# State space parameters in seventeen small steps, and the state space inputs in sixteen transfers

## Chip, core and metric

The kernel runs on one core of a Trainium2 chip. The metric is the device time of one execution in microseconds (us). Before the change the median of three runs is 3636.02 us (3635.19 to 3643.21).

The engines are named as the profile names them: PE is TensorE (matmuls and transposes), PEld its weight loads, DVE is VectorE, ACT is ScalarE, POOL is GpSimd, SP is SyncE, which in this kernel issues every DMA.

## The reference

512 tokens of width 2048 pass through two layers of a first block and one layer of a second block. The change touches only the first block. Each of its layers computes, from x and a condition vector c:

```python
mod = c_act @ w_ada[l] + b_ada[l]                     # shift, scale, gate
h = rms_norm(x, norm_g[l]) * (1 + scale) + shift
u, z_s, q, k, v, z_a = split(h @ w_in[l])             # six parts of width 1024
y_s = s5_mixer(u, ...) * silu(z_s)                    # state space part
y_a = diff_attention(rope(q), rope(k), v) * silu(z_a)
x = x + gate * (concat(y_s, y_a) @ w_out[l])
```

The state space part is a linear recurrence with 64 groups of 16 channels and 64 complex states each:

```python
step = exp(log_step); a_bar = exp(lam * step)
b_bar = ((a_bar - 1) / lam)[..., None] * b_mat
states = scan(a_bar, einsum('gnp,bsgp->bsgn', b_bar, u))
y = einsum('gpn,bsgn->bsgp', c_mat, states).real + d_skip * u
```

followed by a gelu and a gated linear unit. What depends on parameters alone (powers of `a_bar`, their products with B and C) is computed on the chip in each layer, and that computation is what the change moves.

## The kernel before

**Weights.** All large products are fp32 done as three matmuls of a high and a low part. `piece` (L261) loads 512 KB of weights into one of five `raw` buffers, ACT rounds it to `hi` (L266), DVE makes `lo = raw - hi` (L269), and `mm3` or `group_tok` issues 24 matmuls of 512 columns for it: 8 of `hi` with the high activations, 8 of `hi` with the low ones, 8 of `lo`. `piece` also calls, at a set rate, a filler that loads a piece of `w_ada` into `raw` and reduces it on DVE (L515, the "dots").

**Order.** The program is written in the order of priority. A planner then simulates the engines and gives each engine, and the queue of SP, a fixed order of instructions: at each point the instruction of highest priority that is ready by its estimates. On the chip every engine works through its list in order, so one that is late there holds up all behind it, transfers in SP's queue too.

**Layer 0.** `start` computes `u` of layer 0 (pieces of `wuA0`, then, after the loop over `before`, four pieces of `wuB0`) and writes it to DRAM as `u_d`. Then eight pieces of `za` (gate of the attention), eight pieces of `wv` (values, `group_tok`), and eight heads: a block for q (two pieces), one for k, the attention. State space steps are put beside the heads. Layer 1 has the same parts, with `za` in eight blocks of two pieces.

**Parameters** (`ssm_params`). A scalar part (about a hundred DVE instructions on 32 columns) is followed by four quarters `qd`. Each quarter loads its B and C from DRAM (`ssb`, L653) into the one buffer `g[:, 1536:2048]`, and then
- DVE makes `E`, powers times B, in 24 instructions (`powmul`, L664 to L666), into one of two halves of `G[:, 0:8]`;
- POOL negates a part of C (L673), clears `Cb` and copies C into it (L676, L679);
- PE multiplies `Cb` with `E` (L685, 32 small matmuls) into a bank `kp` with tag `tr`; ACT copies it (L688), PE transposes it back into `kp` (L690), DVE copies and completes it (L693 to L699) and eight DMAs store it (`K_d`, L702);
- PE transposes `E` (L708, 16 of them, into the two banks of tag `tr`), ACT copies, four DMAs store (`FT_d`);
- POOL makes `CA`, powers times C, in 24 instructions (again L664 to L666), and four DMAs store it (`CA_d`).

The next quarter's load overwrites the buffer that `CA` reads, and in program order each quarter's POOL work stands behind the one before. `Cb`, `ks`, `k2` and the copies of the transposes share four buffers of tag `p`. In layer 0 the scalar part is called after `start`, and one quarter after each second piece of `za` (`beside`). The parameters of layer 1 are all called at once in layer 0 (`mid`), between the gated linear unit (`glu`) and the output product (eight pieces of `woA`, ten blocks of `wo`, then half blocks).

**Inputs** (`ssm_steps`). Eight DMAs read `u_d` in rows of 64 numbers (256 bytes) into `up = G[:, 0:8]` (L762), all at the first step, which is called after `za` and before `wv`. `E` uses the same part of `G`. Then come eight state steps, which load `FT_d` (L769) into two alternating halves and run 16 matmuls each (L776), the recurrence on POOL (L788 to L791), and eight output steps.

Of the kernel before, what the change touches and what calls it, by code (L numbers as in the profile page):

```python
# [20 lines left out]
KT = 16  # L21
# [146 lines left out]
class Kern:  # L168
# [150 lines left out]

    def group(self, srcs, ns, acts, evac, extra=(), rate=None, halves=0):  # L320


        nk = len(acts)
        pss = [self.bank() for _ in range(4)] + [self.sbank(t, b) for t, b in extra]
        for c, k0 in [(c, k0) for c in HALVES for k0 in range(0, halves, 2)] + [(slice(0, S), k0) for k0 in range(halves, nk, 2)]:
            if k0 == max(halves, 4) and rate is not None:
                self.rate = rate
            base = 0
            for src, n in zip(srcs, ns):
                w = n * 128  # L330
                hi, lo = self.piece(src[:, k0 * w:(k0 + 2) * w], 2 * w)
                self.mm3([(pss[base + m][:, c], slice(k * w + m * 128, k * w + (m + 1) * 128), [a[:, c] for a in acts[k0 + k]],
                           k0 + k == 0 and c.start == 0, k0 + k == nk - 1) for k in range(2) for m in range(n)], hi, lo)
                base += n
        for m in range(base):
            evac(m, pss[m])

    def group_tok(self, src, acts, n, evac, halves=0):

        nk = len(acts)  # L340
        pss = [self.bank() for _ in range(4)]
        per = 1024 // n // 2 * 2
        for tt, k0 in [(tt, k0) for tt in ((0, 1), (2, 3)) for k0 in range(0, halves, per)] + [(range(4), k0) for k0 in range(halves, nk, per)]:
            hi, lo = self.piece(src[:, k0 * n:(k0 + per) * n], per * n)
            for k in range(per):
                mh, ml = acts[k0 + k]
                sl = slice(k * n, (k + 1) * n)
                for t in tt:
                    ts = slice(t * 128, (t + 1) * 128)
                    first, last = k0 + k == 0, k0 + k == nk - 1  # L350
# [3 lines left out]
                    mm(pss[t][:, :n], ml[:, ts], hi[:, sl], start=False, stop=last)  # L354
        for t in range(4):
            evac(t, pss[t])
# [215 lines left out]
    def ssm_params(self, l):  # L572

        nc, I = self.nc, self.I
        g = self.G[:, 8:16, :].rearrange("p a b -> p (a b)")
# [53 lines left out]
        for i in range(4):  # L629
            t = pw[i]  # L630
# [16 lines left out]
        nc.vector.tensor_copy(cf[:, 96:128], ci)  # L647
        T = nc.gpsimd.tensor_tensor
        yield
        for qd in range(4):  # L650
            pa = slice(qd * 8, qd * 8 + 8)
            sbq = g[:, 1536:2048].rearrange("p (k r a c) -> p k r a c", k=2, r=2, a=8)
            nc.sync.dma_start(sbq.rearrange("p k r a c -> p (k r) (a c)"),  # L653
                              I[f"ssb{l}"].rearrange("p (k q c) -> p k q c", k=4, q=4)[:, :, qd])
            sc = self.t2("wt", 1, shape=(128, 1280))
            tm = sc[:, 0:512], sc[:, 512:1024]
            tv = self.t2("n", 4), self.t2("n", 4)

            def powmul(T, tm, out, f, src, n, op=ADD):

                fv = f.rearrange("p (k r a) -> p k r a", k=2, r=2)[:, :, :, pa]
                for r in range(2):
                    t = tm[r][:, :8 * n].rearrange("p (a c) -> p a c", a=8)
                    T(t, fv[:, 1, r].unsqueeze(2).to_broadcast([128, 8, n]), src[:, 1 - r], MUL)  # L664
                    T(out[:, r], fv[:, 0, r].unsqueeze(2).to_broadcast([128, 8, n]), src[:, r], MUL)
                    T(out[:, r], out[:, r], t, op)  # L666
            V = nc.vector.tensor_tensor
            E = self.G[:, 4 * (qd % 2):4 * (qd % 2) + 4, :].rearrange("p a b -> p (a b)").rearrange("p (r a dc) -> p r a dc", r=2, a=8)
            powmul(V, tv, E[:, :, :, 0:16], cf, sbq[:, 0], 16)
            for i, n in enumerate((16, 32, 64)):  # L670
                powmul(V, tv, E[:, :, :, n:2 * n], pw[i], E[:, :, :, 0:n], n)

# [7 lines left out]
            kp = self.sbank("tr", 2)  # L680
# [6 lines left out]
            ks, k2 = self.t2("p", 4), self.t2("p", 4)  # L687
            nc.scalar.copy(k2[:, :256], kp[:, :256])  # L688
            for x in range(2):
                nc.tensor.transpose(kp[:, 256 + 128 * x:384 + 128 * x], k2[:, 128 * x:128 * x + 128], self.ident)  # L690
# [12 lines left out]

            for r in range(2):
                for a0 in range(0, 8, 4):
# [5 lines left out]
                    nc.sync.dma_start(self.FT_d[l][qd * 2 + a0 // 4, r], ft)  # L711

            CA = g[:, 2048:4096].rearrange("p (r a ic) -> p r a ic", r=2, a=8)
            powmul(T, tm, CA[:, :, :, 0:16], pw[0], sbq[:, 1], 16, SUB)
            for i, n in enumerate((16, 32, 64)):
                powmul(T, tm, CA[:, :, :, n:2 * n], pw[i], CA[:, :, :, 0:n], n, SUB)
            for r in range(2):
                for h in range(2):
                    nc.sync.dma_start(self.CA_d[l][qd][64 * r:64 * r + 64, h], CA[64 * h:64 * h + 64, r])
            yield  # L720

    def ssm_param_storage(self):
# [8 lines left out]
        self.K_d = [self.dp.tile([16, 64, 15, 16], F32, name=f"K_d{l}") for l in range(2)]  # L731
        self.u_d = self.dp.tile([1024, 512], F32, name="u_d")

    def ssm_pad(self):
# [19 lines left out]
    def ssm_steps(self, l):  # L754
# [8 lines left out]
        yield  # L763

# [159 lines left out]

    def start(self, hacts, before):

# [28 lines left out]
        for m in range(4):  # L955
            self.ssm_put(m, pa[m], A[:, m, :])
        pb = [self.bank() for _ in range(4)]
        for k0 in (8, 10, 12, 14):
# [4 lines left out]

    def layer(self, l, xsrc, on_x, nxt, after_u=lambda: None, mid=lambda: None, beside=lambda: None):
        nc, I, A, G = self.nc, self.I, self.A, self.G
# [7 lines left out]
        def ev_za(j, ps):  # L973
            self.act(A[:, 8 + j, :], ps, AF.Silu)
        if l:
            self.blocks([wi[24 + j] for j in range(8)], hacts, ev_za)
        else:
            for j in range(8):
# [8 lines left out]
        ssm = self.ssm_steps(l)  # L987
        next(ssm)
        va = A[:, 0:4, :]
        self.group_tok(I[f"wv{l}"][0], hacts, 512, lambda t, ps: nc.scalar.copy(va[:, t, :], ps))  # L990

# [32 lines left out]
        self.rate = (1, 1)[l]  # L1024
        mid()
        yacts = [(self.HH[:, k, :].bitcast(F32R), self.HL[:, k, :].bitcast(F32R)) for k in range(16)]

        def ev_o(m, ps):
            nc.sync.dma_start(A[:, m, :], xsrc[m])
            self.stt(A[:, m, :], ps, self.mod[l][:, 32 + m:33 + m], A[:, m, :], MUL, ADD)  # L1030
            on_x(m)

        def ev_half(m, ps, c):
# [3 lines left out]
            on_x(m, c)  # L1037
        self.group([I[f"woA{l}"]], [4], yacts, ev_o)
        self.blocks([I[f"wo{l}"][j] for j in range(10)], yacts, lambda j, ps: ev_o(4 + j, ps))
        self.rate = 0  # L1040
# [497 lines left out]
def build(ctx, tc, I, O):  # L1538
# [22 lines left out]
    K.start(K.acts(), before)  # L1561
    next(par)
    K.ssm_pad()
    K.rope_tables()
    K.lambdas()
    K.gain_root()
    xs = K.dp.tile([2, KT, 128, 512], F32, name="xs")
# [63 lines left out]

    def mid():
        for _ in K.ssm_params(1):
            pass
    K.layer(0, [I["xT"][m] for m in range(KT)], on_x(0), nxt(0), after_u, mid, lambda: next(par, None))
    K.layer(1, [xs[0, m] for m in range(KT)], on_x(1), nxt(1))
# [18 lines left out]
```

## Time and profile before

| | before |
|---|---|
| median of three runs | 3636.02 us |
| the profiled execution | 3646.28 us |
| its span, first to last instruction | 3644.5 us |
| mean granted TensorE clock, of full speed | 0.969 |
| PE busy | 3442.2 us (94%) |
| DVE busy | 2118.7 us (58%) |
| ACT busy | 1187.5 us (33%) |
| POOL busy | 645.0 us (18%) |

Busy times of the engines overlap. The profiled execution lies 0.3% above the median of the runs, and 1.8 us of it lie outside the span. PE is nearly always busy, so time is gained where PE waits, and where its clock is granted at less than full speed.

### The profile page before, as it was taken

The page shows a single profiled execution, that of the slowest core. Times are in us where ns is not written, and L with a number is a line of the kernel's source. Part 1 is how long each engine was busy: PE and PEld are TensorE (multiplying, and loading weights), DVE is VectorE, ACT ScalarE, POOL GpSimd, SP SyncE. Part 2 cuts the span into 40 slices and gives each one's busy share as a digit, 9 for nine tenths or more (in the row PEclk, how much of TensorE's full clock was granted, in tenths as well). Part 3 has the DMA queues.
Part 4 walks back from the last instruction along what each step waited for, and adds up shares of the span by engine and source line. Part 5 has one row for each costly group of instructions (what it writes and reads, how often), then busy time and mean ns, then how long its engine had stood idle before and what let it go on. Part 6 is the DMA issues. An engine that isn't in the chain of part 4 may idle for free.

```text
span 3644.5 us, 45627 instructions
## 1 busy us (share of the span) xinstructions
PE 3442.2 (94%) x16673; PEld 2740.3 (75%) x16673; DVE 2118.7 (58%) x4157; ACT 1187.5 (33%) x2052; POOL 645.0 (18%) x885
## 2 busy tenths in 40 slices
PE   7987899999779998899999999999999999999999
PEld 4866667778569876677788887887888777788887
DVE  7983555667857334646575589823893246434432
ACT  3422232353124222323433344321532134433311
POOL 0064293001750003920002202000210000000000
PEclk8998999999889999999999999999999999999999
DMA  9856636656566855356577636332333232224442
GB/s 329 286 161 166 187 107 172 193 179 218 176 201 220 220 176 164 112 161 190 172 221 229 196 118 130 113 96 75 101 99 113 72 95 79 70 93 136 145 138 93
DMA packets 264862, 565.04 MB, mean 155 GB/s; under 512 B 76476, under 2 KB 113597, under 8 KB 264637
## 3 DMA queue, kind: packets, MB, share of 16 engines
q1 hardware_dynamic: 264638, 562.14, 50.6%
q8 instruction: 131, 2.15, 0.2%
q14 instruction: 93, 0.76, 0.1%
HBM read 497.89 MB, written 50.50 MB: 150 GB/s over the span
## 4 chain that ended last, share of the span: by engine, by line
PE 58%; DVE 9%; DMA 8%; POOL 4%; issue 3%; SPq 1%; ACT 0%; DVEq 0%; POOLq 0%; ACTq 0%
PE pp L281 16%; PE pp L282 16%; PE pp L284 16%; DMA raw<-in_wada 6%; DVE lo L269 2%; DVE G L249 1%; PE sc L888 1%; DVE raw L515 1%; DVE G L1232 1%; POOL G L791 1%; PE sc L1363 1%; POOL misc L789 1%; PE tr L1290 1%; POOL G L666 1%; SPq L804 1%
## 5 line engine op out<-in xcount | busy, mean ns | idle before, releaser
L281 PE MATMUL pp<-HH,hi 128*128 128x512 f32 (+1 forms) x3568 | 1401.5, 396 | 27.1 <-ACT HH L565 20.9
L282 PE MATMUL pp<-HL,hi 128*128 128x512 f32 (+1 forms) x3440 | 1345.5, 394 | 0.2 <-DVE HL L252 0.2
L266 ACT CAST hi<-raw 128x1024 fp32r<-128x1024 f32 (+1 forms) x538 | 560.5, 1043 | 1196.1 <-PE pp L282 973.8
L284 PE MATMUL pp<-HH,lo 128*128 128x512 f32 (+1 forms) x3568 | 910.9, 393 | 4.9 <-DVE lo L269 4.9
L269 DVE TENSOR_TENSOR lo<-raw,hi 128x1024 fp32r<-128x1024 f32 (+1 forms) x506 | 625.7, 1239 | 355.7 <-PE pp L284 174.7
L281 PEld LDWEIGHTS pp<-HH,hi 128*128 128x128 f32 x3568 | 682.5, 192 | 186.2 <-issue 28.6
L284 PEld LDWEIGHTS pp<-HH,lo 128*128 128x128 f32 x3568 | 663.1, 190 | 157.3 <-issue 18.6
L282 PEld LDWEIGHTS pp<-HL,hi 128*128 128x128 f32 x3440 | 658.0, 191 | 150.5 <-issue 20.2
L515 DVE CUSTOM_DVE_ANT_0 raw<-raw,cs,vec 128x1024 f32<-128x1024 f32 x112 | 155.3, 1388 | 265.1 <-DMA raw<-in_wada 252.7
L515 DVE CUSTOM_DVE_ANT_0 raw<-raw,cs,mod 128x1024 f32<-128x1024 f32 x112 | 146.5, 1308 | 246.9 <-DMA raw<-in_wada 228.4
L217 ACT ACTIVATE p<-p,st 128x128 f32<-128x128 f32 (+2 forms) x192 | 101.9, 531 | 232.0 <-DVE st L244 231.5
L1606 POOL TENSOR_TENSOR rp<-rp,n 128x512 f32<-128x512 f32 (+1 forms) x43 | 65.0, 1526 | 418.2 <-ACT n L1605 418.1
L353 PE MATMUL pp<-lo,HH 128*128 128x512 f32 (+1 forms) x320 | 123.2, 390 | 4.1 <-DVE lo L269 4.1
L352 PE MATMUL pp<-hi,HH 128*128 128x512 f32 (+1 forms) x320 | 122.3, 388 | 3.9 <-ACT HH L565 3.1
L269 POOL TENSOR_TENSOR lo<-raw,hi 128x1024 fp32r<-128x1024 f32 x32 | 77.9, 2434 | 255.5 <-PE pp L284 133.7
L354 PE MATMUL pp<-hi,HL 128*128 128x512 f32 (+1 forms) x320 | 117.3, 388 | 0.9 <-DVE HL L252 0.9
L788 POOL TENSOR_TENSOR misc<-misc,G 128x64 f32<-128x64 f32 x124 | 53.8, 434 | 330.4 <-ACT G L778 321.2
L888 PE MATMUL sc<-rp,rp 64*128 64x512 f32 (+3 forms) x256 | 89.9, 500 | 15.3 <-DVE st L890 15.3
L282 PE MATMUL pp<-A,hi 128*128 128x512 f32 x256 | 100.7, 393 | 0.0
L664 POOL TENSOR_TENSOR wt<-G 128x128 f32<-128x128 f32 (+2 forms) x64 | 65.4, 1041 | 174.9 <-DVE G L631 149.4
L890 DVE CUSTOM_DVE_ANT_0 p<-sc,cst 128x128 f32<-128x128 f32 (+3 forms) x128 | 60.8, 483 | 29.3 <-PE sc L888 29.2
L353 PEld LDWEIGHTS pp<-lo,HH 128*128 128x128 f32 x320 | 63.0, 197 | 18.4 <-DVE lo L269 4.7
(319 smaller groups left out, 3959.8 us busy)
## 6 DMA issues: line engine op xcount, KB each, us to landing
raw<-in_wada SPq DMA_DIRECT2D x224, 512.0 KB, 4.2
raw<-in_w SPq DMA_DIRECT2D x164, 512.0 KB, 3.8
raw<-in_win SPq DMA_DIRECT2D x128, 512.0 KB, 4.7
raw<-in_wo SPq DMA_DIRECT2D x80, 512.0 KB, 4.7
G<-in_wad SPq DMA_DIRECT2D x64, 512.0 KB, 6.0
raw<-in_wv SPq DMA_DIRECT2D x32, 512.0 KB, 3.8
raw<-in_wglu SPq DMA_DIRECT2D x32, 512.0 KB, 4.2
raw<-in_wuA SPq DMA_DIRECT2D x18, 512.0 KB, 5.0
```

What stands on the lines that cost most here:

```text
L217: i = self.nc.scalar.activation(out, src, func, **kw)
L266: nc.scalar.copy(hi[:, :n].bitcast(F32R), raw[:, :n])
L269: eng.tensor_tensor(lo[:, :n].bitcast(F32R), raw[:, :n], hi[:, :n], SUB)
L281: mm(out, hi[:, sl], mh, start=first, stop=False)
L282: mm(out, hi[:, sl], ml, start=False, stop=False)
L284: mm(out, lo[:, sl], mh, start=False, stop=last)
L352: mm(pss[t][:, :n], mh[:, ts], hi[:, sl], start=first, stop=False)
L353: mm(pss[t][:, :n], mh[:, ts], lo[:, sl], start=False, stop=False)
L354: mm(pss[t][:, :n], ml[:, ts], hi[:, sl], start=False, stop=last)
L515: self.nc.vector.tensor_tensor_reduce(w, w, cs, 1.0, self.vec[:, o:o + 1] if first else m, MUL, ADD, m)
L664: T(t, fv[:, 1, r].unsqueeze(2).to_broadcast([128, 8, n]), src[:, 1 - r], MUL)
L888: nc.tensor.matmul(sc[:, :W], q[rows, i * 128:(i + 1) * 128], k[rows, :W], start=True, stop=True)
```

## The change

- `ssm_params` is cut into seventeen steps. The first is the scalar part with `prep(0)`. Each quarter is then four steps: (1) `products` and the first half of the transposes of `E` (`turned`), (2) the second half and `lags` (what follows `kp`), (3) `prep` of the next quarter, that is its load, `E` and `Cb`, and after it `carried`, that is `CA` and its stores, (4) nothing.
- B and C have two buffers in turn; the second one, `sb2`, is new. `kp` takes a bank of tag `sc` instead of `tr`.
- Layer 0: the first step, with the padding, rotation tables and other small constants, moves ahead of the last four pieces of `start` (`late`). One step follows each of the eight pieces of `za` and of the eight of `wv`.
- Layer 1's parameters: the first step stays between `glu` and the output product; one step then follows each `woA` piece from the third on, and each of the ten `wo` blocks.
- The inputs come in sixteen DMAs of half the size. In layer 0 eight go between `wv` pieces, four after them, four behind the first q block; the state steps follow the first k block (four) and the second q block (four, and the recurrence). In layer 1 two follow each `za` block, and the state steps stay where they were.

```diff
+        def prep(qd):
+            sbq = sbqs[qd % 2]
             nc.sync.dma_start(sbq..., I[f"ssb{l}"]...[:, :, qd])
...
+        def products(qd, E, Cb):
+            kp = self.sbank("sc", 2)
...
+        made = prep(0)
+        yield
+        for qd in range(4):
+            k = products(qd, *made)
+            turned(qd, made[0], (0,))
+            yield
+            turned(qd, made[0], (1,))
+            lags(qd, *k)
+            yield
+            if qd < 3:
+                made = prep(qd + 1)
+            carried(qd)
+            yield
             yield
...
-        for d in range(8):
-            src = bass.AP(tensor=ud.tensor, offset=ud.offset + 64 * (7 - d), ap=[[512, 16], [16 * 512, 64], [1, 64]])
-            nc.sync.dma_start(up[16 * d:16 * d + 16], src)
-        yield
+        for x in range(2):
+            for d in range(8):
+                src = bass.AP(tensor=ud.tensor, offset=ud.offset + 64 * (7 - d) + x * 32 * 16 * 512, ap=[[512, 16], [16 * 512, 32], [1, 64]])
+                nc.sync.dma_start(up[16 * d:16 * d + 16, 32 * x:32 * x + 32], src)
+                yield
...
         if l:
-            self.blocks([wi[24 + j] for j in range(8)], hacts, ev_za)
+            for j in range(8):
+                self.blocks([wi[24 + j]], hacts, lambda _, ps: ev_za(j, ps))
+                next(ssm)
+                next(ssm)
...
-                if j % 2 == 0:
-                    beside()
+                next(par)
...
+        ups = iter((0, 0, 0, 1, 1, 2, 2, 2))
+        def beside():
+            next(par)
+            for _ in range(next(ups)):
+                next(ssm)
+        self.group_tok(I[f"wv{l}"][0], hacts, 512, ..., 0, (beside, lambda: None)[l])
+        for _ in range((4, 0)[l]):
+            next(ssm)
...
-            head(h, va, (((2, 1), (3, 3), (0, 0), (0, 0)), ((5, 4), (0, 0), (0, 0), (0, 0)))[l][h])
+            head(h, va, (((4, 4), (5, 0), (0, 0), (0, 0)), ((5, 4), (0, 0), (0, 0), (0, 0)))[l][h])
...
-        mid()
+        next(par_next, None)
...
+        wait = iter((0, 0))
+        self.group([I[f"woA{l}"]], [4], yacts, ev_o, side=lambda: next(par_next, None) if next(wait, 1) else None)
+        for j in range(10):
+            self.blocks([I[f"wo{l}"][j]], yacts, lambda _, ps: ev_o(4 + j, ps))
+            next(par_next, None)
```

## Rows read from the trace of the kernel before

**Rows 1.** Busy time by stretch: stretch, its length, engines (instructions), clock, DMA share, GB/s

```profile
180.00:340.00 160.00, 126.31 (x647) 101.08 (x646) 111.62 (x219) 38.38 (x52) 102.33 (x110) 0.88 0.54 162
340.00:380.00 40.00, 32.36 (x190) 26.95 (x189) 12.22 (x16) 8.68 (x11) 0.62 (x1) 0.87 1.12 205
920.00:1080.00 160.00, 117.66 (x599) 94.22 (x598) 106.99 (x164) 33.49 (x47) 105.89 (x95) 0.86 0.61 187
1090.00:1240.00 150.00, 150.00 (x844) 132.23 (x843) 96.58 (x134) 61.32 (x75) 4.31 (x3) 1.00 0.71 229
1240.00:1340.00 100.00, 92.38 (x387) 75.18 (x386) 36.39 (x44) 22.12 (x24) 0.00 (x0) 0.95 0.74 182
```

**Rows 2.** PE's waits, 180 to 420 us: waiter, releaser, total us, times, longest

```profile
PE tr L685 <- POOL p L679: 19.1, 2, 11.6
PE tr L708 <- DVE p L693: 8.6, 3, 5.4
PE sc L776 <- DMA rp<-rp: 7.6, 1, 7.6
```

**Rows 3.** PE's waits, 800 to 1090 us

```profile
PE tr L708 <- DVE p L693: 12.2, 2, 9.8
PE tr L685 <- POOL p L679: 11.4, 2, 8.1
PE tr L708 <- ACT p L710: 9.5, 2, 4.8
PE tr L685 <- DVE G L666: 7.7, 1, 7.7
```

**Rows 4.** PE's waits, 1240 to 1420 us

```profile
PE sc L776 <- DMA A<-FT_d: 10.2, 1, 10.2
PE pp L353 <- DVE lo L269: 4.1, 1, 4.1
PE pp L284 <- DVE lo L269: 3.5, 2, 2.0
```

**Rows 5.** DVE by line, 180 to 340 us: busy us, mean ns, idle before

```profile
L269 DVE TENSOR_TENSOR lo<-raw,hi 128x1024 fp32r<-128x1024 f32 x19 | 25.1, 1335 | 0.0
L665 DVE TENSOR_TENSOR G<-G 128x128 f32<-128x128 f32 (+2 forms) x32 | 19.0, 596 | 0.0
L666 DVE TENSOR_TENSOR G<-G,n 128x128 f32<-128x128 f32 (+2 forms) x32 | 18.0, 588 | 0.0
L664 DVE TENSOR_TENSOR n<-G 128x128 f32<-128x128 f32 (+2 forms) x32 | 17.4, 575 | 4.4 <-DMA G<-in_ssb 4.4
```

**Rows 6.** POOL by line, 180 to 340 us

```profile
L664 POOL TENSOR_TENSOR wt<-G 128x128 f32<-128x128 f32 (+2 forms) x32 | 34.2, 1088 | 151.2 <-DVE G L631 149.4 <-DVE G L634 1.7
L665 POOL TENSOR_TENSOR G<-G 128x128 f32<-128x128 f32 (+2 forms) x32 | 33.6, 1052 | 2.1 <-DVE G L632 1.2 <-DMA CA_d<-G 0.8
L666 POOL TENSOR_TENSOR G<-G,wt 128x128 f32<-128x128 f32 (+2 forms) x32 | 30.5, 970 | 0.2
```

**Rows 7.** PE in order of time, last matmuls of two pieces: start us, us

```profile
175.72 1.98 PE L284 MATMUL pp<-HH,lo 128*128 128x512 f32 x8
181.16 1.98 PE L284 MATMUL pp<-HH,lo 128*128 128x512 f32 x8
```

**Rows 8.** POOL in order of time, around the last quarter of layer 0

```profile
294.49 0.86 POOL L664 TENSOR_TENSOR wt<-G 128x128 f32<-128x128 f32 x2
...
298.39 8.83 POOL L664 TENSOR_TENSOR wt<-G 128x128 f32<-128x128 f32 x2
...
322.20 0.83 POOL L679 COPY p<-G 64x256 f32<-64x256 f32 x2
```

**Rows 9.** PE in order of time, the same place

```profile
323.09 1.94 PE L685 MATMUL tr<-G,p 128*32 128x128 f32 x32 [11.60 <-POOL p L679]
```

**Rows 10.** SP's queue in order of time, inputs of layer 0

```profile
350.98 11.83 SPq L762 DMA_DIRECT2D G<-u_d  x6
...
367.79 1.02 SPq L265 DMA_DIRECT2D raw<-in_win  x2
```

More of the change, by code (lines that the diff above doesn't have):

```diff
@@ L318, in half_blocks, with group @@
             after(c)
-    def group(self, srcs, ns, acts, evac, extra=(), rate=None, halves=0):
+    def group(self, srcs, ns, acts, evac, extra=(), rate=None, halves=0, side=lambda: None):
         nk = len(acts)
@@ L334, in group, with group_tok @@
                 base += n
+                side()
         for m in range(base):
             evac(m, pss[m])
-    def group_tok(self, src, acts, n, evac, halves=0):
+    def group_tok(self, src, acts, n, evac, halves=0, side=lambda: None):
         nk = len(acts)
@@ L354, in group_tok @@
                     mm(pss[t][:, :n], ml[:, ts], hi[:, sl], start=False, stop=last)
+            side()
         for t in range(4):
@@ L647, in ssm_params, with powmul @@
         nc.vector.tensor_copy(cf[:, 96:128], ci)
-        T = nc.gpsimd.tensor_tensor
-        yield
-        for qd in range(4):
-            pa = slice(qd * 8, qd * 8 + 8)
-            sbq = g[:, 1536:2048].rearrange("p (k r a c) -> p k r a c", k=2, r=2, a=8)
+        T, V = nc.gpsimd.tensor_tensor, nc.vector.tensor_tensor
+        sbqs = [t.rearrange("p (k r a c) -> p k r a c", k=2, r=2, a=8) for t in (g[:, 1536:2048], self.sb2)]
+        def powmul(T, tm, out, f, src, n, qd, op=ADD):
+            fv = f.rearrange("p (k r a) -> p k r a", k=2, r=2)[:, :, :, qd * 8:qd * 8 + 8]
+            for r in range(2):
+                t = tm[r][:, :8 * n].rearrange("p (a c) -> p a c", a=8)
+                T(t, fv[:, 1, r].unsqueeze(2).to_broadcast([128, 8, n]), src[:, 1 - r], MUL)
+                T(out[:, r], fv[:, 0, r].unsqueeze(2).to_broadcast([128, 8, n]), src[:, r], MUL)
+                T(out[:, r], out[:, r], t, op)
@@ L653, in ssm_params @@
+        def prep(qd):
+            sbq = sbqs[qd % 2]
             nc.sync.dma_start(sbq.rearrange("p k r a c -> p (k r) (a c)"),
                               I[f"ssb{l}"].rearrange("p (k q c) -> p k q c", k=4, q=4)[:, :, qd])
-            sc = self.t2("wt", 1, shape=(128, 1280))
-            tm = sc[:, 0:512], sc[:, 512:1024]
             tv = self.t2("n", 4), self.t2("n", 4)
[L659 to L666, printed above, removed]
@@ L679, in ssm_params @@
                 nc.gpsimd.tensor_copy(Cb[rows, :, :, h, :], sbq[rows, 1])
-            kp = self.sbank("tr", 2)
+            return E, Cb
+        def products(qd, E, Cb):
+            kp = self.sbank("sc", 2)
             for x in range(2):
@@ L686, in ssm_params, with lags @@
                                          E[:, r, a], start=r == 0, stop=r == 1)
-            ks, k2 = self.t2("p", 4), self.t2("p", 4)
+            k2 = self.t2("p", 4)
             nc.scalar.copy(k2[:, :256], kp[:, :256])
+            return kp, k2
+        def lags(qd, kp, k2):
+            pa = slice(qd * 8, qd * 8 + 8)
+            ks = self.t2("p", 4)
             for x in range(2):
@@ L702, in ssm_params, with turned @@
                 nc.sync.dma_start(kd[:, :, pa, 7 + d, :], ksv[16 * d:16 * d + 16])
-            for r in range(2):
+        def turned(qd, E, rs):
+            for r in rs:
                 for a0 in range(0, 8, 4):
@@ L711, in ssm_params, with carried @@
                     nc.sync.dma_start(self.FT_d[l][qd * 2 + a0 // 4, r], ft)
+        def carried(qd):
+            sbq = sbqs[qd % 2]
+            sc = self.t2("wt", 1, shape=(128, 1280))
+            tm = sc[:, 0:512], sc[:, 512:1024]
             CA = g[:, 2048:4096].rearrange("p (r a ic) -> p r a ic", r=2, a=8)
-            powmul(T, tm, CA[:, :, :, 0:16], pw[0], sbq[:, 1], 16, SUB)
+            powmul(T, tm, CA[:, :, :, 0:16], pw[0], sbq[:, 1], 16, qd, SUB)
             for i, n in enumerate((16, 32, 64)):
-                powmul(T, tm, CA[:, :, :, n:2 * n], pw[i], CA[:, :, :, 0:n], n, SUB)
+                powmul(T, tm, CA[:, :, :, n:2 * n], pw[i], CA[:, :, :, 0:n], n, qd, SUB)
             for r in range(2):
@@ L923, in start_u, with start @@
         self.group([I[f"wuA{l}"], I[f"wuB{l}"]], [4, 4], hacts, self.ssm_put, [("sc", 2), ("sc", 2), ("tr", 2), ("tr", 2)], 1, 4)
-    def start(self, hacts, before):
+    def start(self, hacts, before, late):
         nc, I, A = self.nc, self.I, self.A
@@ L956, in start @@
             self.ssm_put(m, pa[m], A[:, m, :])
+        late()
         pb = [self.bank() for _ in range(4)]
@@ L961, in start, with layer @@
             self.ssm_put(4 + m, pb[m], A[:, 4 + m, :])
-    def layer(self, l, xsrc, on_x, nxt, after_u=lambda: None, mid=lambda: None, beside=lambda: None):
+    def layer(self, l, xsrc, on_x, nxt, after_u=lambda: None, par=iter(()), par_next=iter(())):
         nc, I, A, G = self.nc, self.I, self.A, self.G
@@ L983, in layer @@
                 self.act(A[:, 8 + j, :], A[:, 8 + j, :], AF.Silu)
-                if j % 2 == 0:
-                    beside()
+                next(par)
         self.rate = (0.75,0.75)[l]
-        ssm = self.ssm_steps(l)
-        next(ssm)
         va = A[:, 0:4, :]
-        self.group_tok(I[f"wv{l}"][0], hacts, 512, lambda t, ps: nc.scalar.copy(va[:, t, :], ps))
+        ups = iter((0, 0, 0, 1, 1, 2, 2, 2))
[3 more added lines that the diff above has]
+                next(ssm)
+        self.group_tok(I[f"wv{l}"][0], hacts, 512, lambda t, ps: nc.scalar.copy(va[:, t, :], ps), 0, (beside, lambda: None)[l])
+        for _ in range((4, 0)[l]):
+            next(ssm)
         def head(h, vt, side):
@@ L1037, in ev_half @@
             on_x(m, c)
-        self.group([I[f"woA{l}"]], [4], yacts, ev_o)
-        self.blocks([I[f"wo{l}"][j] for j in range(10)], yacts, lambda j, ps: ev_o(4 + j, ps))
+        wait = iter((0, 0))
[3 more added lines that the diff above has]
+            next(par_next, None)
         self.rate = 0
@@ L1560, in before, with late @@
             K.make_h(0, rstd, [k])
[L1561 to L1566, printed above, removed]
+    def late():
+        K.ssm_pad()
+        K.rope_tables()
+        K.lambdas()
+        K.gain_root()
+        next(par)
+    K.start(K.acts(), before, late)
     xs = K.dp.tile([2, KT, 128, 512], F32, name="xs")
@@ L1630, in nxt @@
         return f
[L1632 to L1635, printed above, removed]
+    K.layer(0, [I["xT"][m] for m in range(KT)], on_x(0), nxt(0), after_u, par, K.ssm_params(1))
     K.layer(1, [xs[0, m] for m in range(KT)], on_x(1), nxt(1))
```

8 lines of the change are left out of this document (4 added, 4 removed).

## Prediction

> **What bounds the kernel now.** I read the busy table first: PE is busy 94% of the span, so only a stretch in which PE waits, or runs under a lowered clock, can give time back. The view of stretches finds two of 160 us where the parameters are made. In layer 0 (180 to 340 us) PE is busy 126.3 us at a granted clock of 0.88, in layer 1's turn (920 to 1080 us) 117.7 us at 0.86 [rows 1]. So PE stands idle for 33.7 and 42.3 us there, and a clock below 1 adds about 126.3 x 0.12 = 15 and 117.7 x 0.14 = 16 us. Two more places follow the loads of the inputs: 7.6 us idle and 32.4 x 0.13 = 4 us of clock in layer 0 (340 to 380 us), 7.6 us idle and 92.4 x 0.05 = 5 us of clock in layer 1 (1240 to 1340 us) [rows 1]. Together 91 us idle and 40 us of clock: no more than about 131 us can be won.
>
> The view of PE's waits names what ends last. In layer 0 it is twice the copy of C by POOL, 19.1 us, and three times the bank that DVE has not yet emptied, 8.6 us [rows 2]. In layer 1's turn it is the same pair, 11.4 and 12.2 us, then ACT, 9.5 us, and once the end of `E`, 7.7 us [rows 3]. In time the copy ends at 322.2 + 0.8 and the products start at 323.1 after 11.6 us of waiting [rows 8, 9]: the copy stood in POOL's list behind the whole `CA` of the quarter before, because its C could only be loaded when `CA` had read the one buffer. `CA` costs (34.2 + 33.6 + 30.5) / 4 = 24.6 us a quarter [rows 6], `E` (19.0 + 18.0 + 17.4) / 4 = 13.6 us on DVE [rows 5]. A piece of weights is 5.44 us of PE [rows 7].
>
> **The change, part by part.** No instruction of arithmetic is added or dropped; the sum is made of waits.
>
> (1) Copy of C ahead of `CA`, two buffers. The copy is now called two pieces before its products and ahead of the `CA` beside it. What may stand before it is only what is left of the `CA` a quarter (four pieces, 21.8 us) earlier: 24.6 - 21.8 = 3 us a quarter at worst, adding up to 9 us at the last, against 10.9 us of slack. I count all of 19.1 + 11.4 = 30.5 us as removed; the other bound, where POOL falls behind, is in the second rival.
>
> (2) `kp` in another bank, half of the transposes before the lags. The waits of transposes for DVE's emptying of `kp` go: 8.6 + 12.2 = 20.8 us. Both banks of tag `sc` are free in these stages, since no attention runs. If a bank were short, these come back.
>
> (3) `E` of layer 1's first quarter gets three `woA` pieces, 16.3 us, in front of its products: the 7.7 us go, and the second `E`, which stood before those pieces' `lo` on DVE, comes after. In layer 0 `late` puts the scalar part and `E` before the `lo` of four pieces; DVE has next to no idle time ahead of such instructions [rows 5], so it is full in either order and a wait is shifted rather than made. I count zero, bounded by 2 x 5.44 us of loss (two pieces that wait for their `lo`) and the same of gain (`E` earlier).
>
> (4) The wait for ACT, 9.5 us: ACT empties banks between other work that waits for POOL. POOL's work stays, so I take half, 4.8 us; bounds 0 and 9.5.
>
> (5) Clock. Idle time and lost clock come together in these rows, so I let the clock return in the share of the idle time removed. Layer 0: 27.7 of 33.7 us, so 12 of 15 us; layer 1: 11.4 + 12.2 + 7.7 + 4.8 = 36.1 of 42.3 us, so 14 of 16.
>
> (6) What takes the place of these waits. In layer 0 DVE needs 111.6, POOL 102.3 and PE 126.3 x 0.88 = 111 us of the 160 [rows 1]. In the 130 us that the sum leaves, DVE and PE would each be 86% full; coupled in order they won't run without waits. With `E` at 13.6 us and two `lo` of 1.3 us against a slack of 10.9 us, each of three quarters can be 5.3 us late: up to 16 us if no `E` starts early, zero if all do. I take 10 off. In layer 1's turn the later steps have 10.9 us of PE each, so nothing is full; I take 10 off for the first quarter and POOL's other work. So 27.7 + 12 - 10 = 30 us in layer 0, 36.1 + 14 - 10 = 40 us in layer 1's turn.
>
> (7) Inputs. Six of the eight issues hold SP's queue for 11.8 us, and the weights behind them are issued 16.8 us after the first [rows 10]. Halved and spread, SP is held about 1 us at a time and five `raw` buffers bridge that. Total bytes and their 256 byte rows stay, and DMA has room: a share of 0.71 in the 150 us where layer 1 will load them [rows 1]. Layer 1 gains 7.6 + 5 us, of which I take 8 (the 10.2 us wait for `FT_d` [rows 4] isn't touched). Layer 0 gains 7.6 + 4 us, but now four state steps stand in a row on two buffers, as in layer 1 where that wait of 10.2 us arises; I take 2 us. Bounds: 24 us gained, 10 us lost.
>
> (8) The planner orders the whole kernel anew, so some other place gets a wait. I take off one of the longest kind seen, 11.6 us [rows 9], and a little clock: 14 us. Below nothing this is bounded by -14 (as likely to drop one).
>
> Sum: 30 + 40 + 8 + 2 - 14 = 66 us. The profiled execution would fall from 3646 to 3580 us. The median of the runs lies 10 us lower, so I forecast 3636 - 66 = **3570 us**. About 0.2% (7 us) is what a measurement of this kernel can tell from no change.
>
> One rule speaks against part (6). Two POOL instructions of one kind took 0.86 us at one place and 8.83 us at another, while DVE was at work [rows 8]; the blocked time is already in the 24.6 us. The Trainium skill, "SBUF — State Buffer", section "Who interferes with whom", says that VectorE and GpSimd share a port pair as an exclusive lock, which a VectorE instruction with two SBUF inputs (`E` and `lo` are such) takes against GpSimd's reads, the loser blocking entirely. The trace agrees as far as those rows go. By that rule taken strictly, the two would add up in layer 0, 111.6 + 102.3 = 214 us; the 160 us that they took show that they partly overlap, yet closer packing may not pay.
>
> **Rivals.**
>
> *DVE and POOL already fill layer 0.* If packed work on one slows the other, the 160 us of layer 0 stay, and PE's waits only change their names. Then 30 us are lost from the sum: 3600 us. For it: the 8.83 us above, and 112 and 102 us of busy time. Against: rows 2 show POOL waited for only as the last of a chain that the single buffer made, and DVE is idle for 48, POOL for 58 of the 160 us [rows 1].
>
> *Everything comes back.* No allowance of parts (6) and (8), bounds of (4) and (7): 27.7 + 12 + 36.1 + 4.8 + 14 + 12 + 12 = 119 us; taking four fifths of it, 95 us, gives 3541 us. For it: all steps in layer 1's turn have ample slack. Against: such tight lists were late by up to 11.6 us at single stops before.
>
> *More stops in PE's list: slower.* The products, the two halves of the transposes and the lags are now at least three stops per quarter among the pieces, 24 in the eight quarters. The planner's estimates set their places; where `E`, a `p` buffer or a store in SP's queue is late on the chip, PE and the weights behind stand still each time. The 131 us of today over 24 stops are 5.5 us each; the change loses when the mean new stop with its clock is dearer than that. At 6 us: 24 x 6 - 131 = 13 us lost, 3649 us. For it: single stops of 4.8 to 11.6 us [rows 2, 3]. Against: today's stops have two named causes, which the change takes away.
>
> *Moved, not saved.* Layer 0's earlier end is absorbed by later state steps behind the first k block, layer 1's by POOL's adds: within 7 us of 3636.
>
> **How the numbers follow.** Forecast (3550 to 3590) 0.50; layer 0 full (3590 to 3615) 0.23; everything (below 3550) 0.13; moved 0.05; slower 0.09. So faster 0.86, same 0.05, slower 0.09. The range for 8 in 10 runs from 3545, which cuts off most of the third case, to 3612, which takes in most of the second.
>
> **What would show it.** Right: in the waits of PE the products no longer wait for L679's counterpart, nor transposes for the copy out of `kp`; both 160 us stretches shrink, by about 30 and 40 us, and their clock rises over 0.93; no stretch of SP's queue is filled by input loads alone. Wrong: PE waits for `E` or for POOL at each products, busy times of POOL and DVE in layer 0 grow by over a tenth, or the state steps wait longer for `FT_d` than 10.2 us.

## The result, and the profile after

The kernel after takes 3600.27 us (median of four runs, 3597.03 to 3605.87), the kernel before on the same chip 3635.81 us. The ratio is 0.9899, with a 95% interval of 0.9881 to 0.9917: 36 us faster, 30 us less than forecast. That is inside the range (3545 to 3612), but in the stretch of the rival "DVE and POOL already fill layer 0" (3590 to 3615, given 0.23) and not in that of the forecast (3550 to 3590, given 0.50). All ratios here compare undisturbed runs of the two kernels on one chip.

The busy time by stretch of the kernel after, columns as in [rows 1]:

```profile
180.00:340.00 160.00, 139.76 (x751) 112.79 (x750) 120.78 (x220) 41.70 (x57) 105.16 (x109) 0.93 0.68 192
340.00:380.00 40.00, 34.81 (x216) 24.51 (x212) 23.38 (x57) 11.26 (x24) 2.38 (x1) 0.91 0.63 200
920.00:1080.00 160.00, 138.41 (x732) 113.17 (x733) 106.63 (x143) 39.84 (x56) 81.39 (x78) 0.89 0.69 213
```

PE is idle for 20 instead of 34 us in layer 0, and for 22 instead of 42 us in this window of layer 1's turn (partly because the turn now begins 25 us earlier: over the same weight matmuls, below, it is 32 instead of 42 us). The clock rose from 0.88 to 0.93 and from 0.86 to 0.89. DVE and POOL have no less to do than before.

In the kernel after, `E` and `CA` are made in L659 to L661, C is copied in L679, the products are L688, the transposes of `E` L718 and the input loads L792. What PE waits for: first from 180 to 420 us, as [rows 2], then from 800 to 1090 us, as [rows 3]; columns are waiter, releaser, total, times, longest.

```profile
PE tr L718 <- ACT p L720: 7.6, 1, 7.6
PE sc L688 <- POOL p L679: 6.0, 1, 6.0
PE pp L281 <- DVE n L249: 5.6, 1, 5.6
PE sc L806 <- DMA A<-FT_d: 5.2, 1, 5.2
...
PE sc L688 <- DVE G L661: 20.1, 4, 13.2
PE pp L284 <- DVE lo L269: 8.1, 4, 4.4
```

The waits that the change was to remove are nearly gone: the copy of C (now L679) 6.0 instead of 30.5 us, the copy out of `kp` none instead of 20.8 us. In layer 1's turn `E` (now L659 to L661) has taken their place: 20.1 us, of which 13.2 in one stop.

To see where time was gained I set the two traces against each other by the count of weight matmuls that PE has done, each stretch taken from its first weight matmul to the first behind it. Of the 45.3 us between the two spans (10 us more than between the medians, since the execution profiled of before was a long one), 18.1 lie in `za` and `wv` of layer 0 (141.4 to 123.3 us), 9.3 behind them in its eight heads, 13.0 in `woA` and `wo` of layer 0 (layer 1's turn, 222.2 to 209.2 us), 4.9 in `za` of layer 1. The stretch ahead of `za` of layer 0 is 4.9 us longer; the rest is small and of both signs. PE's idle time fell from 31.0 to 14.6 us in the first of these stretches and from 42.3 to 32.3 us in layer 1's turn.

SP's queue in order of time, beside [rows 10], first the longest row of input loads in layer 0, then that in layer 1:

```profile
317.80 3.24 SPq L792 DMA_DIRECT2D G<-u_d  x6
...
1202.23 12.69 SPq L792 DMA_DIRECT2D G<-u_d  x8
```

In layer 0 no input loads fill the queue for 12 us any more. In layer 1 they still do: the planner put eight of the halved loads in a row.

### The profile page after: what moved, and what is told of

The parts are those of the page before. It is cut to its first block, busy times and chain, and to the rows that moved or that the text cites. A ratio compares the mean times of both kernels' runs of the same rounds, so it can differ in the third digit from the quotient of the medians.

```text
span 3599.2 us, 45635 instructions
## 1 busy us (share of the span) xinstructions
PE 3432.1 (95%) x16673; PEld 2728.0 (76%) x16673; DVE 2128.8 (59%) x4157; ACT 1185.8 (33%) x2052; POOL 633.5 (18%) x885
## 4 chain that ended last, share of the span: by engine, by line
PE 67%; DVE 11%; DMA 9%; POOL 8%; issue 3%; SPq 1%; ACT 1%; DVEq 0%; POOLq 0%; ACTq 0%
PE pp L282 18%; PE pp L281 18%; PE pp L284 18%; DMA raw<-in_wada 5%; DVE lo L269 2%; PE sc L918 1%; POOL misc L820 1%; POOL G L821 1%; POOL misc L818 1%; DVE G L249 1%; POOL misc L819 1%; DVE raw L517 1%; POOL lo L269 1%; POOL G L660 1%; PE sc L1407 1%
## 5 line engine op out<-in xcount | busy, mean ns | idle before, releaser
L284 PEld LDWEIGHTS pp<-HH,lo 128*128 128x128 f32 x3568 | 659.9, 190 | 162.6 <-issue 19.8
L517 DVE CUSTOM_DVE_ANT_0 raw<-raw,cs,mod 128x1024 f32<-128x1024 f32 x112 | 154.6, 1381 | 248.6 <-DMA raw<-in_wada 245.3
L918 PE MATMUL sc<-rp,rp 64*128 64x128 f32 (+3 forms) x256 | 92.6, 493 | 10.4 <-DVE st L920 10.4
L353 PEld LDWEIGHTS pp<-hi,HH 128*128 128x128 f32 x320 | 61.9, 194 | 17.7 <-ACT HH L567 3.9
```

The source lines that it names most:

```text
L284: mm(out, lo[:, sl], mh, start=False, stop=last)
L517: self.nc.vector.tensor_tensor_reduce(w, w, cs, 1.0, self.vec[:, o:o + 1] if first else m, MUL, ADD, m)
L918: nc.tensor.matmul(sc[:, :W], q[rows, i * 128:(i + 1) * 128], k[rows, :W], start=True, stop=True)
```

## The experiments

The question is why the waits that were named went and only half of their time came back. **Theory** (formed from the profile after): POOL's `CA` and DVE's `E` run side by side and slow each other, so whatever order the steps have, `E` or `Cb` is late. **Rivals**: DVE has too much work of its own (dots, `lo`, two quarters of `E` at once); it is the spreading of the steps; it is the inputs; or a part of the change costs what another gives.

### Parts of the change by themselves

**inputs_only**: the kernel before with the sixteen transfers and their places; the parameters as they were.

```diff
+            for j in range(8):
+                self.blocks([wi[24 + j]], hacts, lambda _, ps: ev_za(j, ps))
+                next(ssm)
+                next(ssm)
...
+        def feed():
+            for _ in range(next(ups)):
+                next(ssm)
+        self.group_tok(..., 0, (feed, lambda: None)[l])
```

> The kernel before, with the sixteen input transfers and their places alone; the parameters stay as they were. By the trace of after (the heads 0 to 3 of layer 0 are 3 us shorter and those of layer 1 6 us shorter than before) the inputs are worth 4 to 10 us: 3626 to 3632 us, a ratio of 0.997 to 0.999. My forecast of part (7) was 10 us. Rival, inputs were hidden anyway: 3636 us, and what those heads gained came from the parameters. Rival, four state steps in a row cost more than the shorter holds of SP's queue give: over 3640 us.

Ratio 0.9972 (0.9960 to 0.9985), some 10 us. The sum of part (7) holds; by the count of weight matmuls (explained above) `za` of layer 1 is 5.8 us shorter, and in layer 0 the first four heads are 5.7 us shorter and `wv` ahead of them 5.2 us longer.

**params_only**: the kernel after, inputs as before.

```diff
-        for x in range(2):
-            for d in range(8):
-                ...[32 groups of 64]; yield
+        for d in range(8):
+            ...[64 groups of 64]
+        yield
```

> The kernel after, with the inputs again as eight transfers at one step (in layer 0 behind the wv pieces, in layer 1 behind za, state steps where they were before). If the two parts add up, this takes 36 us less what the run with the inputs alone gains: 3604 to 3610 us, ratio 0.991 to 0.993. Rival, the input part costs where it meets the parameters in layer 0 (SP, DVE): as fast as after or faster, 3600 us or less.

Ratio 0.9924 (0.9912 to 0.9936), 28 us. 10 + 28 = 38 us against 36: the parts add up, so what is missing is missing from the parameters.

**layer1_at_once**: layer 1's steps all behind the gated linear unit.

```diff
-        next(par_next, None)
+        for _ in par_next:
+            pass
```

> The kernel after, with all steps of layer 1's parameters called at once behind the gated linear unit, as before; two buffers, the other bank and layer 0 stay. Theory, E is late and DVE is slowed by POOL's CA beside it: spreading matters little for those, and the two buffers with the other bank alone keep most of the 16 us of this stretch: 3603 to 3610 us. Rival, spreading the steps is what gave the 16 us: 3614 to 3620 us. Rival, spreading brought the 13.2 us wait for E and nothing else: faster than after, 3590 us.

Ratio 0.9882 (0.9869 to 0.9896): as fast as after, if not faster, and faster than the 3603 to 3610 us that I expected. The spreading in layer 1's turn gives nothing. PE's waits of this run, 860 to 1080 us:

```profile
PE sc L688 <- DVE G L661: 13.5, 2, 13.2
PE sc L688 <- POOL p L679: 13.0, 1, 13.0
```

The stop for the first `E` is 13.20 us, as in after; the second is another one of 13.0 us, for POOL. `woA` and `wo` take 208.3 us here and 209.2 us in after, so the order of the steps isn't what sets their length.

**late_undone**: the scalar part behind `start`, as before.

```diff
-    K.start(K.acts(), before, late)
+    K.start(K.acts(), before, lambda: None)
+    late()
```

> The kernel after, with the scalar part and the small constants called behind start again, as before, and not ahead of its last four pieces. I counted this as zero: 3597 to 3604 us. Rival, it makes E of the first quarter early enough: undone, layer 0 has a wait for E as long as the 13.2 us of layer 1, 3608 us or more. Rival, it holds up lo of the four pieces: undone, faster by up to 10 us.

Ratio 0.9908 (0.9893 to 0.9923), which can't be told from after.

**one_buffer**: part (1) undone.

```diff
-        sbqs = [... for t in (g[:, 1536:2048], self.sb2)]
+        sbqs = [... for t in (g[:, 1536:2048], g[:, 1536:2048])]
...
+            carried(qd)
             if qd < 3:
                 made = prep(qd + 1)
-            carried(qd)
```

> The kernel after, with one buffer for B and C instead of two, and CA of a quarter again ahead of the next quarter's load, E and Cb. By part (1) of the prediction the waits for the copy of C come back, 30.5 us with their clock: 3630 to 3640 us, ratio 0.997 to 1.000. Theory after the runs without CA: the second buffer also let CA run beside E, so E becomes faster again and only a part comes back: ratio 0.993 to 0.997. Rival, the other bank for kp and the spreading gave the gain: as after, 0.989 to 0.991.

Ratio 0.9893 (0.9874 to 0.9912): no loss, so both expectations of a loss failed and the rival's number came. PE's waits, 160 to 420 us and then 840 to 1090 us:

```profile
PE sc L688 <- DVE G L661: 8.0, 2, 7.3
PE sc L688 <- POOL p L679: 6.3, 1, 6.3
...
PE sc L688 <- DVE G L661: 19.3, 5, 7.7
PE tr L718 <- DVE G L661: 7.7, 1, 7.7
```

In layer 1's turn it stops for `E` no less than with two buffers. The copy of C is waited for 6.3 us and not 30.5 us, so it was not the second buffer that took that wait away. (In this one trace `za` and `wv` are 9.9 us longer than in after, and several other stretches a few us shorter; in the total nothing is left of it.)

**kp_in_tr**: the bank of part (2) undone.

```diff
-            kp = self.sbank("sc", 2)
+            kp = self.sbank("tr", 2)
```

> The kernel after, with kp again in a bank of tag tr, beside the transposes. By part (2) the transposes wait for DVE's emptying of kp again, 20.8 us in the kernel before: ratio 0.994 to 0.997, and waits of transposes for the copy out of kp show. Rival, with the lags now a step of their own the two banks suffice: ratio 0.989 to 0.991 and no such waits.

Ratio 0.9896 (0.9879 to 0.9913), the rival's number, and no wait for the copy out of `kp` shows. So the bank is not what took that wait away; the rival, that it was the step of its own for `lags`, fits but was not tested by itself. (1) and the bank of (2), each undone alone, cost nothing.

### POOL beside DVE

**no_ca**: the price of `CA`'s arithmetic; a memset in its place.

```diff
-            powmul(T, tm, CA[:, :, :, 0:16], pw[0], sbq[:, 1], 16, qd, SUB)
-            for i, n in enumerate((16, 32, 64)):
-                powmul(T, tm, CA[:, :, :, n:2 * n], pw[i], ...)
+            nc.gpsimd.memset(CA, 0.0)
```

> The kernel after, without the arithmetic of CA on POOL in both layers: one memset takes the place of its 24 instructions a quarter, the stores stay (so the output lacks the part that CA carries). It prices what POOL's work beside E costs. Theory, E is late because POOL slows DVE: E's instructions on 128x512 take 0.6 instead of 1.1 to 1.4 us, the wait of 13.2 us for E in layer 1's turn falls under 5 us, and the DVE time of layer 0 between 180 and 300 us falls by over 10 us; ratio 0.982 to 0.986 (after: 0.990). Rival, DVE is full by its own work (dots, lo, two quarters of E at once): the wait for E stays over 9 us, ratio 0.988 to 0.991.

Ratio 0.9745 (0.9725 to 0.9765), 93 us under before, more than I expected. DVE by line from 800 to 1150 us, `E` alone, first of after and then of this run (busy us, mean ns, idle before):

```profile
L661 DVE TENSOR_TENSOR G<-G,n 128x128 f32<-128x128 f32 (+2 forms) x32 | 19.8, 645 | 0.0
L660 DVE TENSOR_TENSOR G<-G 128x128 f32<-128x128 f32 (+2 forms) x28 | 17.7, 640 | 2.5 <-PE tr L718 2.5
L659 DVE TENSOR_TENSOR n<-G 128x128 f32<-128x128 f32 (+2 forms) x28 | 16.4, 624 | 0.0
```

```profile
L661 DVE TENSOR_TENSOR G<-G,n 128x128 f32<-128x128 f32 (+2 forms) x32 | 12.6, 425 | 0.0
L659 DVE TENSOR_TENSOR n<-G 128x128 f32<-128x128 f32 (+2 forms) x28 | 12.1, 470 | 0.0
L660 DVE TENSOR_TENSOR G<-G 128x128 f32<-128x128 f32 (+2 forms) x28 | 11.9, 435 | 2.4 <-PE tr L718 2.4
```

The same 88 instructions take 36.6 instead of 53.9 us. Between 180 and 300 us DVE is busy for 89.4 instead of 106.9 us. PE's longest wait for `E` in layer 1's turn is 2.3 us:

```profile
PE sc L688 <- DVE G L661: 2.3, 1, 2.3
```

The rival that DVE is full by its own work falls: dots, `lo` and two quarters of `E` are all still there. In the kernel before the three lines took 55 us in this span (96 instructions), so the slowing is not new. Not all of the 93 us need be the slowing of `E`: without `CA`, POOL's list is also shorter, and the copy of C, 6.0 us in after, is not waited for.

**ca_after_e**: all work done, but `CA` of a quarter held on POOL until the next quarter's `E` is done.

```diff
+            last = E[:, :, 7, 127:128]
+            nc.gpsimd.tensor_copy(sc[:, :1024].rearrange("p (r c) -> p r c", r=2)[:, :, 0:1], last)
+            nc.gpsimd.tensor_copy(CA[:, :, 0, 0:1], last)
             powmul(T, tm, CA[:, :, :, 0:16], pw[0], sbq[:, 1], 16, qd, SUB)
```

> The kernel after, with each quarter's CA held until the E of the next quarter is done: two tiny POOL copies read E's last elements and write a first element of CA and of its temporaries. All work is done. Theory, POOL beside E is what makes E late: the 13.2 us wait falls under 6 us and that time is not lost again, since nobody waits for CA soon; ratio 0.984 to 0.988. Rival, POOL falls behind in layer 0, where a quarter has 21.8 us of PE and CA costs 24.6: products wait for the copy of C again, as in rows 2, 10 us or more; ratio 0.991 to 0.995. Rival, DVE full by its own work: same as after, wait over 9 us.

Ratio 0.9811 (0.9792 to 0.9829), 69 us under before and 32 us under after, more than I expected. DVE has the same list in both kernels where layer 1's first `E` ends, so time can be compared instruction by instruction. First DVE and then POOL of after, in order of time (start us, us):

```profile
898.53 1.02 DVE L249 TENSOR_TENSOR G<-G 128x32 f32<-128x32 f32 x1
899.48 0.17 DVE L244 TENSOR_SCALAR misc<-G 128x32 f32<-128x32 f32 x1
899.56 1.27 DVE L637 COPY misc<-G 128x32 f32<-128x32 f32 x1
...
924.95 5.71 DVE L661 TENSOR_TENSOR G<-G,n 128x512 f32<-128x512 f32 x4
```

```profile
895.30 4.20 POOL L660 TENSOR_TENSOR G<-G 128x512 f32<-128x512 f32 x2 [1.62 <-DVE G L635]
...
923.90 2.02 POOL L660 TENSOR_TENSOR G<-G 128x512 f32<-128x512 f32 x1
925.89 3.40 POOL L661 TENSOR_TENSOR G<-G,wt 128x512 f32<-128x512 f32 x2
```

DVE of the kernel with the hold, the same instructions, and POOL's first instruction after 66.89 us of waiting (L730 is the hold):

```profile
878.66 0.18 DVE L249 TENSOR_TENSOR G<-G 128x32 f32<-128x32 f32 x1
878.77 0.17 DVE L244 TENSOR_SCALAR misc<-G 128x32 f32<-128x32 f32 x1
878.85 0.17 DVE L637 COPY misc<-G 128x32 f32<-128x32 f32 x1
...
894.18 2.48 DVE L661 TENSOR_TENSOR G<-G,n 128x512 f32<-128x512 f32 x4
```

```profile
896.82 1.03 POOL L730 COPY wt<-G 128x2 f32<-128x2 f32 x1 [66.89 <-DVE G L661]
```

From the start of L249 to the end of the four L661 it is 924.95 + 5.71 - 898.53 = 32.1 us with `CA` beside, and 894.18 + 2.48 - 878.66 = 18.0 us without. The difference of 14.1 us is about as long as the stop of 13.20 us that `E` costs PE in after (the stop ends with the first of the four; up to there the difference is 11.8 us). PE at the same products, first after, then this run:

```profile
926.62 0.65 PE L688 MATMUL sc<-G,p 128*32 128x128 f32 x8 [13.20 <-DVE G L661]
```

```profile
895.62 0.42 PE L688 MATMUL sc<-G,p 128*32 128x128 f32 x8
```

`woA` falls from 69.5 to 47.8 us, and `wo`, beside which `CA` now runs, takes 139.3 instead of 139.7 us. POOL does not fall behind in layer 0: `za` and `wv` take 114.8 instead of 123.3 us. The conflict is not gone, it has moved: in this turn PE still waits 7.2 us for `E` and 9.3 us for `lo`. One of these stops is in the half blocks behind `wo`, which take 7.4 us longer than in after: there a dot on DVE took 4.45 us beside the late `CA` (1.27 us at 877.46 us in the same trace), and the `lo` behind it came late:

```profile
1040.10 4.45 DVE L517 CUSTOM_DVE_ANT_0 raw<-raw,cs,vec 128x1024 f32<-128x1024 f32 x1 [15.51 <-DMA raw<-in_wada]
...
1046.41 2.07 PE L284 MATMUL pp<-HH,lo 128*128 128x256 f32 x8 [5.22 <-DVE lo L269]
```

**e_in_turn**: the load of the next quarter held until this quarter's `E` is done; `CA` stays free.

```diff
+            if Ep is not None:
+                nc.vector.tensor_copy(sbq[:, 0, :, 0, 0:1], Ep[:, :, 7, 127:128])
             nc.sync.dma_start(sbq..., I[f"ssb{l}"]...)
```

> The kernel after, with the load of the next quarter's B and C held until this quarter's E is done (a tiny DVE copy reads E's last elements and writes an element of the buffer, which the load overwrites), so that two quarters of E can't interleave on DVE. CA stays free to run beside. Theory, the second buffer lets E of quarter 1 run between the instructions of E of quarter 0 and that is half of the wait: E is done some 6 us earlier, the 13.2 us wait falls to 5 to 8 us, ratio 0.987 to 0.989. Rival, it is POOL alone: the wait stays over 11 us. Rival, E of quarter 1 is late instead, by the latency of the load: same time, other name.

Ratio 0.9888 (0.9869 to 0.9907), as after. PE's waits, 840 to 1090 us (the lines of this kernel stand two further down):

```profile
PE sc L690 <- DVE G L661: 21.5, 5, 8.4
PE sc L690 <- POOL p L681: 10.1, 1, 10.1
```

The longest stop is shorter, their sum is not. That two quarters of `E` interleave is no cause of the total.

**both_gates**: the edits of `ca_after_e` and `e_in_turn` together.

> The kernel after with both holds: E of the quarters in turn, CA behind the E of the next quarter. If both causes add up, the wait for the first E goes below 3 us, ratio 0.982 to 0.986. Rival, the chain load, E, CA, load becomes too long in layer 0: slower than after, 0.992 or more.

Ratio 0.9860 (0.9837 to 0.9884), slower than the hold of `CA` alone. The longest wait for `E` was still 6.3 us, so the causes did not add up; which part of the longer chain cost the time I did not separate.

### Moving CA to the other engine

**ca_on_dve**: the kernel after, with this in `carried`.

```diff
-            powmul(T, tm, CA[:, :, :, 0:16], pw[0], sbq[:, 1], 16, qd, SUB)
+            powmul(V, tm, CA[:, :, :, 0:16], pw[0], sbq[:, 1], 16, qd, SUB)
...
-                powmul(T, tm, CA[:, :, :, n:2 * n], pw[i], CA[:, :, :, 0:n], n, qd, SUB)
+                powmul(V, tm, CA[:, :, :, n:2 * n], pw[i], CA[:, :, :, 0:n], n, qd, SUB)
```

> The kernel after, with CA's 24 instructions a quarter on DVE instead of POOL; nothing is left out. If the two engines slow each other, DVE does CA in the time of E alone (38 to 40 us for four quarters without CA, so some 39 us for CA, where POOL took 92 to 97), and E, lo and the dots get back the 17 us a layer that CA cost E: DVE has 20 us more a layer, at places where it has room. Ratio 0.978 to 0.985. Rival, DVE is full from 180 to 245 us and in layer 1's turn: CA's 39 us come on top there, PE waits for lo and E: 0.99 or more.

Ratio 0.9796 (0.9779 to 0.9813), 74 us under before, the fastest version with all its work, though not separable from `ca_after_e`. Busy time by stretch:

```profile
180.00:340.00 160.00, 145.35 (x822) 117.31 (x822) 125.95 (x320) 43.94 (x60) 13.77 (x13) 0.96 0.73 204
920.00:1080.00 160.00, 155.14 (x928) 134.15 (x928) 126.54 (x233) 54.74 (x76) 36.21 (x21) 0.98 0.73 223
```

The busy table of the page, first of after and then of this run:

```profile
PE 3432.1 (95%) x16673; PEld 2728.0 (76%) x16673; DVE 2128.8 (59%) x4157; ACT 1185.8 (33%) x2052; POOL 633.5 (18%) x885
```

```profile
PE 3426.1 (96%) x16673; PEld 2727.8 (76%) x16673; DVE 2134.1 (60%) x4349; ACT 1186.7 (33%) x2052; POOL 464.5 (13%) x693
```

192 instructions moved from POOL to DVE. POOL lost 169 us of busy time, DVE gained 5.

**before_ca_on_dve**: the same two edits, `T` to `V`, in the kernel before, and nothing else.

> The kernel before, with CA on DVE instead of POOL and nothing else: the parameters in four whole quarters, one buffer, kp in tr, eight input transfers. It tells whether the small steps still give something once the two engines no longer slow each other. Theory, POOL beside DVE is one limit and the order of the steps another: the gain of CA on DVE is about that in the kernel after (10 thousandths), ratio 0.987 to 0.992, and the steps with it give 0.980. Rival, the waits that the steps took away were POOL's anyway (C's copy behind CA): the steps add little, ratio 0.979 to 0.984. Rival, with one buffer, CA on DVE stands between two quarters of E: no gain or slower, 0.997 or more.

Ratio 0.9848 (0.9828 to 0.9868), 55 us under before: that alone gives more than the whole change (0.9899). With the change it is 0.9796, so the change still adds 5 thousandths (19 us). The ratio lies between what my theory and the first rival gave. In the two traces the gain of the steps lies in layer 1's turn (`woA` and `wo` take 187.5 us with the change and 202.4 us without), while `za` and `wv` of layer 0 are longer with it (108.0 against 96.9 us). So a part of the waits that the steps were to remove was POOL's anyway, a part was not: PE's longest waits in layer 1's turn of this run, 840 to 1110 us, are

```profile
PE tr L685 <- POOL p L679: 13.1, 2, 11.7
PE pp L281 <- DVE A L252: 10.2, 1, 10.2
```

## Why the prediction was right, and where it was not

The direction and the range hold; the sum of 66 us was too high by 30. The waits were named rightly, but what stood behind them, POOL's `CA` and DVE's `E` slowing each other, was not in the sum.

- **(1)** The copy of C is waited for 6.0 instead of 30.5 us. But that is not what the second buffer was worth: undone, the time is the same. Counting a wait as gained because its releaser is moved was wrong; the next to arrive was `E`, just as late.
- **(2)** The wait for the emptying of `kp` is gone, though not by the bank. Its 20.8 us of time did not all come back: layer 1's turn, where 12.2 of them and 11.4 of (1) lay, is 13.0 us shorter in all.
- **(3)** `E` of layer 1's first quarter was to lose its 7.7 us and waits 13.2. Three pieces in front are 16.3 us of PE, but the DVE list that ends with it took 32.1 us beside `CA` instead of 18.0. That `late` is worth nothing was right.
- **(4)** The waits for ACT in layer 1's turn are gone, and one of 7.6 us came in layer 0.
- **(5)** The clock came back by less than the idle time, to 0.93 and 0.89, not over 0.93 in both. By the prediction's own formula the loss is now 139.8 x 0.07 = 9.8 and 138.4 x 0.11 = 15.2 us, where it was 15.2 and 16.5: some 7 of the 26 us counted. This term was as far off as the waits, and it went with the idle time that stayed: in `no_ca`, where PE is idle for 1.1 us between 180 and 300 us, the clock there is 1.00.
- **(6)** This is the step that failed, by its size, and it took (5) with it. I took off 10 us in each layer for what takes the place of the waits. The waits less this allowance were 27.7 + 36.1 - 20 = 44 us; PE's idle time over the same weight matmuls fell by 16.4 + 10.0 = 26 us. For the parameters the forecast was 30 + 40 - 14 = 56 us with the allowance of (8); the run with the parameters alone gave 28. I had `E` at 13.6 us a quarter and `CA` at 24.6 from [rows 5, 6], as if these were what the work costs. They were the price of doing both at once: without `CA`, `E` takes 39.7 / 4 = 9.9 us (36.6 us of the three lines above, and 3.1 of eight instructions with the new buffer). In after the durations held on the average, because the overlap stayed, but not at the stop of layer 1's turn (32.1 instead of 18.0 us, see (3)). The kernel before had rows that told it: the same instruction took 0.67 us while POOL got nothing done (the 8.83 us of [rows 8]), and 1.74 us beside POOL's `CA`.

```profile
303.58 0.67 DVE L665 TENSOR_TENSOR G<-G 128x512 f32<-128x512 f32 x1
...
951.01 1.74 DVE L665 TENSOR_TENSOR G<-G 128x512 f32<-128x512 f32 x1
```

- **(7)** 10 us forecast, 10 measured with that part alone, but the mechanism held in layer 0 only. In layer 1 the loads still fill SP's queue for 12.69 us, which the prediction had ruled out. That `za` of layer 1 became 4.9 us shorter all the same fits the pause of its weights in SP's queue, 14.4 us (1201.42 to 1215.82 us) where it was 19.8 us (1237.48 to 1257.31 us); this was not tested.
- **(8)** No new wait of the size allowed for shows elsewhere (the largest loss is the 4.9 us ahead of `za` of layer 0), so most of the allowance of 14 us was not needed. It hid a part of the error in (6).

Of the rivals, "DVE and POOL already fill layer 0" gave the time, 3600 us, and the mechanism. That the time fits so well is luck: this rival lost all 30 us of layer 0 and none elsewhere, while the traces show 18 of the 30 us of layer 0 gained, and only 13 of the 40 of layer 1's turn, where I had held that nothing is full. Busy shares over 160 us don't show it. In stretches of 20 us, columns as in [rows 1], the kernel after has DVE full (20.00 of 20 us) just where the first `E` of layer 1 is made:

```profile
900.00:920.00 20.00, 10.42 (x44) 7.62 (x42) 20.00 (x29) 2.11 (x2) 18.60 (x21) 0.96 0.51 154
920.00:940.00 20.00, 10.10 (x56) 7.33 (x57) 20.00 (x19) 3.53 (x7) 18.72 (x19) 0.53 0.64 203
```

"More stops: slower" did not occur, and what "Everything comes back" forecast (95 us) came only without `CA` (93 us).

What I cited of the Trainium skill, "SBUF — State Buffer", section "Who interferes with whom", an exclusive lock between VectorE and GpSimd, agrees with 32.1 against 18.0 us. The sum of busy times that I held against its strict reading (214 us of work in 160 us) was no test of it: a busy time in the profile holds the time in which an instruction is blocked, as the 8.83 us of [rows 8] do, so such a sum counts blocked time on both engines.

Left open: how the missing 30 us divide between the slowing of `E` and late copies of C, and what limits `ca_after_e` and `ca_on_dve` next, which was read from their waits and not tested.

## What to carry to other kernels

A duration read beside another engine's work can include that engine; before you price a step by it, find one row of the same instruction with the other engine silent. When several waits of one chain have different names, removing the names one by one may change nothing: take the suspected common cause away first, here with `CA` left out. And work put on a second engine to relieve the first can cost both: two edits that moved `CA` to DVE gave more than all of the new order.

## What the hardware showed that I had not expected

- Even small DVE instructions can wait out POOL's: the 32-column L249 took 1.02 instead of 0.18 us and ended at 899.55, 0.05 us after POOL's pair had ended (895.30 + 4.20 = 899.50); the 32-column copy after it took 1.27 instead of 0.17 us.
- It goes the other way too, and for longer than one instruction: the POOL pair of [rows 8] that took 8.83 us, against 0.86 us elsewhere, began at 298.39 us and ended at 307.22 us, and DVE worked without a gap until 306.60 us (its next instruction starts at 311.98 us).
- `CA` takes POOL 93 us in layer 1's turn of after. On DVE, `E` and `CA` together take 82 us there, against 57 us for `E` alone beside POOL and 40 without `CA`: DVE does `CA` in some 42 us, and 17 of these had been lost to the overlap already.
